# The inversion of each recurrence pair traced 6 to 10 weight units later, its transfers on GpSimd's queue

## The chip, the core and the metric

One core of one Trainium2 chip. The metric is the device time of one execution in microseconds, the median of three runs. The engines are TensorE (PE; its weight loads run beside it as PEld), VectorE (DVE), ScalarE (ACT), GpSimd (POOL) and SyncE (SP), whose queue issues the kernel's DMAs. Each engine works through its own list of instructions in order.

## What is computed

Two transformer blocks, one after the other, on 256 tokens of width 2048, in float32. The first block's mixer has a stick-breaking attention, a forgetting attention and a recurrence of 16 heads of 64 with a decay, and a gated sum of the three; an MLP follows. The second block has pooling, a latent attention, a memory attention and a gated convolutional MLP. The change touches the recurrence only:

```python
def frame(state, inp):
    r_t, w_t, k_t, v_t, kk_t, kka_t = inp
    sa = jnp.einsum('bhvk,bhk->bhv', state, kk_t)
    state = (state * w_t[:, :, None, :] - sa[..., None] * kka_t[:, :, None, :]
             + v_t[..., None] * k_t[:, :, None, :])
    return state, jnp.einsum('bhvk,bhk->bhv', state, r_t)
```

## The kernel before

**Products.** Nearly all time goes into products of the 256 tokens with weights that are read once. A weight unit is 128 x 1024 float32 (512 KB): `load` (L214) has SP fetch it into `raw`, ACT copy its high part to `hi` (L227) and DVE compute the rest `lo = raw - hi` (L228). Each of the three has three buffers. `lin_t` (L232) goes over output columns in steps of 256 and, within them, over units of four 128-row slices; each slice takes a matmul with `hi` (512 columns, both parts of the tokens) and one with `lo` (256). `lin_n` (L264) is the same with tokens as rows. Results stand in PSUM banks `m` (four) until an eviction takes them (`halves`, L287: ACT writes `hv`, DVE adds). Everything else on PE uses four further banks `s` (`side`, L155).

**Order.** The code is traced in program order; a planner then lays out a list for each engine by readiness and priority, where the trace order is the priority and the weight copies of `load` go far ahead (L226). On the chip an engine follows that list, whatever is ready.

**The recurrence.** `rwkv(q)` (L710) does a quarter of the heads: three products (k, r, v; twelve units), then two pairs of heads in `rwkv_pair` (L368), each with two chunks of 128 tokens for two heads, so four 128 x 128 systems. A pair has

- a head (L372 to L433): decays by scan and exponentials (`cs`, `E`, `Ei`), the scaled operands `AR`, `Bt`, `Kt`, their transposes, and four score matrices into `SM`;
- `k.flush()` (L435), which traces the finish of the pair before;
- the inversion: DVE masks the 16 x 16 diagonal blocks into `X` and reduces them to `mc` (L444, L446). SP writes `mc` to a DRAM tile `md` (32 KB, L448) and reads it back broadcast to all partitions as `mb` (512 KB, L450), after `md` has landed. Fifteen steps `zw`, `zc` on DVE (L454 to L457) invert the blocks, L458 spreads them into `Z`; transposes and small matmuls on PE with copies on ACT and DVE between them (L459 to L495) extend that to 128 x 128;
- the rest: two chunks `R`, `U`, `ys` (L498 to L532), the bonus `pb`, `y2` and the gate `pg`, `gg` (L535 to L543);
- `finish` (L545), which normalises `ys` and writes `yc`.

Tiles have one buffer unless `bufs` says otherwise: `X`, `Z`, `zc`, `mb`, `rk`, `kk` have one, `SM`, `AR`, `vt` two.

**Around it.** The quarters stand between other products: rwkv(0), an attention (24 units, then its softmax), rwkv(1), the other attention, rwkv(2), branch(0) (40 units), rwkv(3), flush, then branch(1) (40 units) and branch(2) (L750 to L800). PE can take the products that follow in the trace while a pair waits.

Of the kernel before, what the change touches and what calls it, by code (L numbers as in the profile page):

```python
# [10 lines left out]
F32 = mybir.dt.float32  # L11
# [113 lines left out]
class K:  # L125
    def __init__(self, ctx, tc):
        self.tc, self.nc, self.ctx = tc, tc.nc, ctx
        nc = tc.nc
        self.v, self.a, self.g, self.pe = nc.vector, nc.scalar, nc.gpsimd, nc.tensor
        pool = lambda name, bufs, **k: ctx.enter_context(tc.tile_pool(name=name, bufs=bufs, **k))  # L130
        self.cp = pool("cp", 1)
        self.wr = pool("wr", 3)
        self.wh = pool("wh", 3)
        self.wl = pool("wl", 3)
        self.ev = pool("ev", 2)
        self.dp = pool("dp", 2, space=bass.MemoryType.DRAM)
# [4 lines left out]
        self.finish = None  # L141
# [24 lines left out]
    def tt(self, out, a, b, op):  # L166
        self.v.tensor_tensor(out=out, in0=a, in1=b, op=op)  # L167
# [46 lines left out]
    def load(self, parts, kt, nc_):  # L214

        raw = self.wr.tile([P, 1024], F32, tag="raw", name=self.nm("raw"), align_bytes=LINE)
        hi = self.wh.tile([P, 1024], F32R, tag="hi", name=self.nm("hi"), align_bytes=LINE)
        lo = self.wl.tile([P, 1024], F32R, tag="lo", name=self.nm("lo"), align_bytes=LINE)
        r3 = raw[:, : kt * nc_].rearrange("p (k n) -> p k n", k=kt)
        h3 = hi[:, : kt * nc_].rearrange("p (k n) -> p k n", k=kt)  # L220
        l3 = lo[:, : kt * nc_].rearrange("p (k n) -> p k n", k=kt)
        for c, ap in parts:
            n = ap.shape[1]
            self.nc.sync.dma_start(r3[:, :, c : c + n], ap.rearrange("(k p) n -> p k n", p=P))
        rr, hh, ll = raw[:, : kt * nc_], hi[:, : kt * nc_], lo[:, : kt * nc_]
        with self.tc.high_priority(offset=3000):  # L226
            self.act(hh, rr, AF.Copy)  # L227
            self.tt(ll, rr, hh.bitcast(F32), ALU.subtract)  # L228
        return h3, l3


    def lin_t(self, w, x, kts, cols, evac, row0=0, xk0=0, segs=None):  # L232
# [7 lines left out]
        for c0, width in cols:  # L240
            ntile = (width + P - 1) // P
            banks = [self.pm.tile([P, 512], F32, tag="m", name=self.nm("m")) for _ in range(ntile)]
            for k0, kt in kts:
# [6 lines left out]
                for j in range(ntile):  # L250
                    m = min(P, width - j * P)
                    for k in range(kt):
# [7 lines left out]
                                start=False, stop=last)  # L260
            for j in range(ntile):
                evac((c0, j), min(P, width - j * P), banks[j])

    def lin_n(self, w, x, kts, cols, evac, row0=0, xk0=0):  # L264


        for c0, width in cols:
            banks = [self.pm.tile([P, 512], F32, tag="m", name=self.nm("m")) for _ in range(2)]
            step = max(1, 1024 // width)
            for k0 in range(0, kts, step):  # L270
# [3 lines left out]
                for t in range(2):  # L274
                    o = banks[t][:, :width]
                    for k in range(kt):
# [42 lines left out]
def rwkv_quarter(k, pool, q, zk, lw, sg1, sg2, w_up, a_up, g_up, yc):  # L319
# [40 lines left out]
    def pairs(zr, zv):  # L360
        for j in range(2):
# [6 lines left out]
def rwkv_pair(k, tl, j, zr, zk, zv, sg, aa, rin, omka, col, gu1, gu2, sg1, sg2, yc):  # L368

# [31 lines left out]
    eif = Ei.rearrange("p c t -> p (c t)")  # L401
    k.stt(Bt, kk, 1.0 / SC, eif, ALU.mult, ALU.mult)
# [3 lines left out]
    k.stt(Kt, kp, 1.0 / SC, eif, ALU.mult, ALU.mult)  # L406
    rk = tl([P, 256], "rk")
# [12 lines left out]
    KT0 = tl([P, P], "KT0")  # L420
    BT0 = tl([P, P], "BT0")
# [13 lines left out]
    k.flush()  # L435
# [4 lines left out]
    Z = tl([P, 4, P], "Z")  # L440
# [11 lines left out]
    zc = tl([P, 4, NB], "zc")  # L452
    k.v.tensor_copy(zc, C["eyeb"].unsqueeze(1).to_broadcast([P, 4, NB]))
    for u in range(NB - 1):  # L454
        w = tl([P, 4, NB], "zw", bufs=2)[:, :, u + 1 :]
        k.tt(w, mb[:, u, :, u + 1 :], zc[:, :, u : u + 1].to_broadcast([P, 4, NB - 1 - u]), ALU.mult)
        k.tt(zc[:, :, u + 1 :], zc[:, :, u + 1 :], w, ALU.subtract)  # L457
    k.tt(blocks(Z), zc.unsqueeze(2).to_broadcast([P, 4, P // NB, NB]), bm, ALU.mult)  # L458
    px = k.side()  # L459
    for i in range(4):  # L460
        k.tp(px[:, i * P : (i + 1) * P], Z[:, i])
    k.act(flat(X), px, AF.Copy)


    half = lambda z, n, o: z.rearrange("p a (b o n) -> p a b o n", o=2, n=n)[:, :, :, o, :]
    wide = lambda z, n: z.rearrange("p (a b n) -> p a b n", a=4, n=n)
    xe, zo, te = half(X, NB, 0), half(Z, NB, 1), half(k.T, NB, 0)
    pt = k.side()[:, :256]
    for i in range(4):
        k.mm(pt[:, i * 64 : (i + 1) * 64], SM[:, i, 0, :], xe[:, i])  # L470
    k.tt(te, wide(pt, NB), C["lev16"].unsqueeze(1).to_broadcast([P, 4, 64]).rearrange("p a (b n) -> p a b n", n=NB),
         ALU.mult)
# [24 lines left out]

    ys = tl([P, 4, 64], "ys", bufs=2)  # L498
    S0 = tl([P, P], "S0")
    k.v.memset(S0, 0.0)  # L500
    for c in range(2):
        pr = k.side()
        if c == 1:
            k.mm(pr[:, :P], AR[:, 1, 0, :], S0, start=True, stop=False)
        for e in range(2):
            i, hs = 2 * c + e, slice(64 * e, 64 * e + 64)
            k.mm(pr[:, hs], SM[:, i, 2, :], vt[:, c, hs], start=c == 0, stop=c == 0 or e == 1)
        R = tl([P, P], "R")
        k.act(R, pr[:, :P], AF.Copy)
        pu = k.side()  # L510
        for e in range(2):
            hs = slice(64 * e, 64 * e + 64)
            k.mm(pu[:, hs], Z[:, 2 * c + e], R[:, hs])
        U = tl([P, P], "U")
        k.act(U, pu[:, :P], AF.Copy)
        if c == 0:
            pS = k.side()
# [10 lines left out]
        for e in range(2):
            i, hs = 2 * c + e, slice(64 * e, 64 * e + 64)
            k.mm(py[:, hs], SM[:, i, 3, :], vt[:, c, hs], start=c == 0, stop=False)  # L530
            k.mm(py[:, hs], SM[:, i, 1, :], U[:, hs], start=False, stop=c == 0 or e == 1)
        k.act(ys[:, 2 * c : 2 * c + 2].rearrange("p e d -> p (e d)"), py[:, :P], AF.Copy)  # L532


    pb = k.side()  # L535
    k.mm(pb[:, :256], brk, rk)
    y2 = tl([P, 256], "y2", bufs=2)
    k.tt(y2, pb[:, :256], zv, ALU.mult)
    pg = k.side()
    k.mm(pg[:, :256], gu1, sg1, start=True, stop=False)  # L540
    k.mm(pg[:, :256], gu2, sg2[:32], start=False, stop=True)
    gg = tl([P, 256], "gg", bufs=2)
    k.act(gg, pg[:, :256], AF.Copy)  # L543

    def finish():  # L545
# [115 lines left out]
def mixer(k, a, xhl):  # L661
# [651 lines left out]
```

## Time and profile before

| | us |
|---|---|
| median of 3 runs | 2752.08 (2749.4 to 2753.53) |
| the profiled execution | 2750.6 |
| its span, first to last instruction | 2748.4 |

The profile is of one execution. Busy time of PE is modelled from pipelined matmuls. A row of a table by windows gives, after its length, the busy time of PE, PEld, DVE, ACT and POOL. PEclk is the share of TensorE's full clock that was granted, over the stretch. "Idle before" is the time an engine stood before an instruction, and the releaser is what it waited for. The line of an instruction is often that of a helper (L160 matmul, L164 transpose, L167 tensor_tensor, L179 activation), so the tile names tell more.

### The profile page before, as it was taken

To read this page: it belongs to the slowest core of one execution; us is meant where nothing else is said; L and a number is where in the kernel's file an instruction comes from. 1 tells how busy PE (TensorE), PEld (TensorE's weight loads), DVE (VectorE), ACT (ScalarE), POOL (GpSimd) and SP (SyncE) were. 2 spreads that over 40 slices of the span, in tenths; PEclk is the share of its full clock that TensorE was granted. 3 is DMA by queue.
4 is the path that set the end of the run, shared out by engine and by line. 5 is a ranking of instruction groups with operands and counts; after the bars stand their busy time and mean duration, and the time that the engine had idled before them with its cause. 6 is when DMAs were issued, how large, how long until landed. Compare 5 with 4: busy or idle time off the path is not lost.

```text
span 2748.4 us, 38434 instructions
## 1 busy us (share of the span) xinstructions
PE 2682.7 (98%) x14588; PEld 2261.9 (82%) x14588; DVE 1734.2 (63%) x2985; ACT 1390.1 (51%) x2245; POOL 37.1 (1%) x36
## 2 busy tenths in 40 slices
PE   7999999999999999999999999999999999999999
PEld 6777787887888888888888888878788888888887
DVE  5657576567666566455565555757767567757764
ACT  7345364453555664444344444766655445535543
POOL 0000000000000000000000000000000000000000
PEclk9999999999999999999999999999999999999999
DMA  6445444464566756665665665554456566666655
GB/s 186 131 130 141 111 128 129 143 168 126 152 189 208 263 175 186 192 191 187 195 186 192 191 185 194 178 155 134 135 163 186 192 190 185 189 194 185 188 187 183
DMA packets 390232, 475.69 MB, mean 173 GB/s; under 512 B 20112, under 2 KB 306832, under 8 KB 390048
## 3 DMA queue, kind: packets, MB, share of 16 engines
q1 hardware_dynamic: 390016, 473.18, 56.6%
q8 instruction: 114, 1.87, 0.3%
q14 instruction: 70, 0.57, 0.1%
q0 software_dynamic: 32, 0.07, 0.0%
HBM read 470.82 MB, written 2.36 MB: 172 GB/s over the span
## 4 chain that ended last, share of the span: by engine, by line
PE 81%; issue 5%; DVE 5%; DMA 3%; ACT 1%; POOL 0%; SPq 0%; POOLq 0%; DVEq 0%; ACTq 0%
PE m L160 75%; PE s L160 5%; DMA mb<-md 2%; DVE lo L167 2%; PE s L164 1%; ACT hi L179 1%; DVE zw L167 1%; DVE zc L167 1%; DMA mt<-in_mem 0%; DMA mt<-in_memT 0%; DVE SM L167 0%; DVE Z L167 0%; POOL rs L196 0%; DVE zz L167 0%; DMA raw<-in_w_in 0%
## 5 line engine op out<-in xcount | busy, mean ns | idle before, releaser
L167 DVE TENSOR_TENSOR lo<-raw,hi 128x1024 fp32r<-128x1024 f32 (+1 forms) x874 | 1062.8, 1217 | 757.8 <-ACT hi L179 754.5
L179 ACT ACTIVATE hi<-raw 128x1024 fp32r<-128x1024 f32 (+1 forms) x874 | 919.9, 1053 | 1040.6 <-PE m L160 793.2
L160 PE MATMUL m<-uhl,hi 128*128 128x512 f32 (+1 forms) x1456 | 528.4, 403 | 2.4 <-DVE zz L167 2.4
L160 PE MATMUL m<-x3hl,hi 128*128 128x512 f32 x1408 | 497.8, 399 | 0.0
L160 PE MATMUL m<-uhl,lo 128*128 128x256 f32 (+1 forms) x1456 | 419.2, 288 | 13.5 <-DVE lo L167 13.5
L160 PE MATMUL m<-x3hl,lo 128*128 128x256 f32 x1408 | 395.5, 281 | 0.0
L160 PE MATMUL m<-A,hi 128*128 128x512 f32 x1024 | 362.0, 399 | 1.8 <-DVE A L170 1.8
L160 PEld LDWEIGHTS m<-uhl,hi 128*128 128x128 f32 (+1 forms) x1456 | 277.0, 190 | 65.8 <-DVE zz L167 3.4
L160 PEld LDWEIGHTS m<-x3hl,hi 128*128 128x128 f32 x1408 | 264.6, 188 | 66.1
L160 PE MATMUL m<-hi,B 128*128 128x512 f32 x1024 | 315.9, 389 | 0.0
L160 PEld LDWEIGHTS m<-uhl,lo 128*128 128x128 f32 (+1 forms) x1456 | 277.8, 191 | 17.5 <-DVE lo L167 15.1
L160 PE MATMUL m<-A,lo 128*128 128x256 f32 x1024 | 287.3, 281 | 0.0
L160 PEld LDWEIGHTS m<-x3hl,lo 128*128 128x128 f32 x1408 | 266.0, 189 | 0.1
L160 PEld LDWEIGHTS m<-A,hi 128*128 128x128 f32 x1024 | 192.0, 188 | 49.2 <-DVE A L170 2.4
L160 PEld LDWEIGHTS m<-hi,B 128*128 128x128 f32 x1024 | 192.2, 188 | 40.0
L160 PE MATMUL m<-hi,h 128*128 128x512 f32 x704 | 217.4, 389 | 0.0
L160 PE MATMUL m<-lo,B 128*128 128x512 f32 x512 | 199.2, 389 | 0.0
L160 PEld LDWEIGHTS m<-A,lo 128*128 128x128 f32 x1024 | 193.3, 189 | 0.8 <-DVE lo L167 0.2
L160 PEld LDWEIGHTS m<-hi,h 128*128 128x128 f32 x704 | 132.1, 188 | 27.6
L179 ACT ACTIVATE hv<-m 128x256 f32<-128x256 f32 x323 | 119.8, 373 | 56.2 <-PE m L160 53.6
L167 DVE TENSOR_TENSOR zz<-m,hv 128x256 f32<-128x256 f32 x307 | 126.8, 417 | 17.6 <-ACT hv L179 17.6
L160 PE MATMUL m<-lo,h 128*128 128x512 f32 x352 | 137.0, 389 | 0.0
(373 smaller groups left out, 3011.1 us busy)
## 6 DMA issues: line engine op xcount, KB each, us to landing
raw<-in_w_in SPq DMA_DIRECT2D x220, 512.0 KB, 3.6
raw<-in_w_mlp_up SPq DMA_DIRECT2D x128, 512.0 KB, 3.6
raw<-in_w_mlp_down SPq DMA_DIRECT2D x128, 512.0 KB, 3.7
raw<-in_w_gate SPq DMA_DIRECT2D x88, 512.0 KB, 3.5
raw<-in_w_up SPq DMA_DIRECT2D x88, 512.0 KB, 3.6
raw<-in_w_down SPq DMA_DIRECT2D x88, 512.0 KB, 3.6
raw<-in_w_out SPq DMA_DIRECT2D x32, 512.0 KB, 4.6
raw<-in_w_o SPq DMA_DIRECT2D x32, 512.0 KB, 3.6
```

Of the source, the lines that this page charges most:

```text
L160: self.pe.matmul(out, lhsT=lhsT, rhs=rhs, start=start, stop=stop)
L164: self.pe.transpose(out, in_, self.C["ident"][:n, :n])
L167: self.v.tensor_tensor(out=out, in0=a, in1=b, op=op)
L179: self.a.activation(out, in_, f, **k)
```

## The change

`rwkv_pair` keeps the head, then traces `pb`, `pg`, the mask and reduction and the two DMAs, now issued by GpSimd. All that follows becomes `solve()`, which is put on a list (`defer`) and traced after 6 further weight units for the first pair of a quarter and 10 for the second; a `tick()` after each unit of `lin_t` and `lin_n` counts down. Only the front of the list is looked at, so the first pair's finish is traced right after the second pair's solve, and the second's a unit later. `pairs` begins with `drain()`. The first `zc` is held behind the split `lo` of the unit traced last. `mb`, `KT0`, `BT0` get two buffers; `Ei` is written over `cs`, `rk` over `kk`, and the bonus goes straight to `yc`. The closing of the recurrence's pool moves behind branch(1).

```diff
-    def flush(self):
-        if self.finish is not None:
-            f, self.finish = self.finish, None
-            f()
+    def defer(self, units, f):
+        self.later.append([units, f])
+    def tick(self):
+        for e in self.later:
+            e[0] -= 1
+        while self.later and self.later[0][0] <= 0:
+            self.later.pop(0)[1]()
+    def drain(self):
+        while self.later:
+            self.later.pop(0)[1]()
...
+            self.last_lo = self.tt(ll, rr, hh.bitcast(F32), ALU.subtract)
...
+                self.tick()
...
     def pairs(zr, zv):
+        k.drain()
...
-    Ei = tl([P, 2, P], "Ei")
...
+    Ei = cs[:, :, 1:]
+    for c in range(2):
+        k.act(Ei[:, c], Ei[:, c], AF.Exp, scale=KAPPA, bias=bp[:, 1, c : c + 1])
...
-    rk = tl([P, 256], "rk")
+    rk = kk
...
-    KT0 = tl([P, P], "KT0")
-    BT0 = tl([P, P], "BT0")
+    KT0 = tl([P, P], "KT0", bufs=2)
+    BT0 = tl([P, P], "BT0", bufs=2)
...
-    k.flush()
+    pb = k.side()
+    k.mm(pb[:, :256], brk, rk)
+    k.tt(yc, pb[:, :256], zv, ALU.mult)
+    pg = k.side()
...
-    k.nc.sync.dma_start(md.rearrange("b (u n) -> (b u) n", u=NB), flat(mc))
-    mb = tl([P, NB, 4, NB], "mb")
-    k.nc.sync.dma_start(mb.rearrange("p u a t -> p (u a t)"),
+    k.nc.gpsimd.dma_start(md.rearrange("b (u n) -> (b u) n", u=NB), flat(mc))
+    mb = tl([P, NB, 4, NB], "mb", bufs=2)
+    k.nc.gpsimd.dma_start(mb.rearrange("p u a t -> p (u a t)"),
                         md.unsqueeze(1).to_broadcast([P // NB, NB, NB * 4 * NB]))
...
+    def solve():
+        zc = tl([P, 4, NB], "zc")
+        with k.tc.issue_after(k.last_lo.ins):
+            k.v.tensor_copy(zc, C["eyeb"].unsqueeze(1).to_broadcast([P, 4, NB]))
...
+        k.defer(1, lambda: finish(ys))
...
-    k.finish = finish
+    k.defer(6 + 4 * j, solve)
...
     rwkv(3)
-    k.flush()
-    rst.close()
     branch(1, a["w_branch_b"][0], ybT, 4)
+    k.drain()
+    rst.close()
```

## Rows read from the trace of the kernel before

**Rows 1.** The page: span, and busy time of each engine (share of the span).

```profile
span 2748.4 us, 38434 instructions
...
PE 2682.7 (98%) x14588; PEld 2261.9 (82%) x14588; DVE 1734.2 (63%) x2985; ACT 1390.1 (51%) x2245; POOL 37.1 (1%) x36
```

**Rows 2.** Windows by stage: from:to, length, busy us by engine (x count), PEclk, DMA.

```profile
75.00:195.00 120.00, 109.78 (x703) 89.79 (x702) 70.06 (x175) 45.45 (x79) 2.16 (x2) 0.97 0.45 124
...
235.00:360.00 125.00, 116.42 (x750) 95.14 (x748) 77.98 (x202) 48.14 (x89) 2.09 (x2) 0.97 0.46 125
...
398.00:512.00 114.00, 104.63 (x697) 87.57 (x696) 74.16 (x199) 46.15 (x90) 1.13 (x2) 0.94 0.45 125
512.00:598.00 86.00, 85.62 (x492) 73.86 (x491) 52.73 (x85) 47.43 (x78) 2.60 (x2) 1.00 0.61 174
598.00:715.00 117.00, 107.51 (x729) 89.32 (x728) 79.76 (x201) 49.88 (x96) 2.09 (x2) 0.97 0.45 124
```

**Rows 3.** Waits of PE, 75 to 715: us in total, times, longest.

```profile
PE m L160 <- DVE lo L167: 18.5, 8, 4.8
PE s L164 <- DVE Z L167: 14.4, 7, 3.3
```

**Rows 4.** Waits of DVE, 75 to 715.

```profile
DVE zw L167 <- DMA mb<-md: 41.3, 8, 7.1
```

**Rows 5.** Timeline of DVE, pair 0: start, us, instruction [idle before <-releaser].

```profile
86.86 1.05 DVE L446 TENSOR_REDUCE mc<-X 128x64 f32<-128x512 f32 x1
...
89.69 1.22 DVE L167 TENSOR_TENSOR lo<-raw,hi 128x1024 fp32r<-128x1024 f32 x1 [0.65 <-ACT hi L179]
...
92.48 1.23 DVE L167 TENSOR_TENSOR lo<-raw,hi 128x1024 fp32r<-128x1024 f32 x1 [1.22 <-ACT hi L179]
98.32 0.22 DVE L167 TENSOR_TENSOR zw<-mb,zc 128x60 f32<-128x60 f32 x1 [4.62 <-DMA mb<-md]
...
100.17 1.22 DVE L167 TENSOR_TENSOR lo<-raw,hi 128x1024 fp32r<-128x1024 f32 x1
...
109.23 1.22 DVE L167 TENSOR_TENSOR lo<-raw,hi 128x1024 fp32r<-128x1024 f32 x1
```

**Rows 6.** Timeline of SP's queue, same place: issues.

```profile
87.94 0.35 SPq L448 DMA_DIRECT2D md<-mc  x1
89.07 0.37 SPq L224 DMA_DIRECT2D raw<-in_w_in  x1
89.50 0.71 SPq L450 DMA_DIRECT2D mb<-md  x1
```

**Rows 7.** Timeline of PE, same place.

```profile
101.44 0.38 PE L160 MATMUL m<-uhl,lo 128*128 128x256 f32 x1 [1.26 <-DVE lo L167]
...
109.36 0.66 PE L164 MATMUL s<-idt,Z 128*128 128x128 f32 x4 [3.35 <-DVE Z L167]
```

**Rows 8.** Windows of 24 us after mc, pairs 4 and 7.

```profile
410.70:434.70 24.00, 19.31 (x99) 16.63 (x98) 14.44 (x42) 9.96 (x14) 0.00 (x0) 0.86 0.56 147
...
666.00:690.00 24.00, 19.98 (x111) 16.57 (x111) 19.39 (x55) 10.49 (x17) 0.00 (x0) 1.00 0.58 156
```

**Rows 9.** Tile rx, 58 to 142 (first and last start); DVE in a window.

```profile
L160 PE MATMUL s<-idt,rx x8: 272/275/377, 75.5 to 131.2; 128*128 128x128 f32 x8
L391 DVE COPY rx<-rin x4: 219/221/226, 63.2 to 78.8; 128x128 f32<-128x128 f32 x4
...
129.80:140.30 10.50, 8.57 (x24) 1.00 0.18 51
```

**Rows 10.** DMA issues by line: count, KB each, median us from issue to landing.

```profile
wua<-in_rwkv_w_up SPq DMA_DIRECT2D x4, 64.0 KB, 2.2
wua<-in_rwkv_a_up SPq DMA_DIRECT2D x4, 64.0 KB, 4.5
...
grow<-in_rows POOLq DMA_DIRECT2D x1, 64.0 KB, 3.9
```

**Rows 11.** Waits of SP's queue, 75 to 715.

```profile
SPq L448 <- DVE mc L446: 43.8, 6, 9.9
```

More of the change, by code (lines that the diff above doesn't have):

```diff
@@ L140, in __init__ @@
         self.abufs = 1
-        self.finish = None
+        self.later = []
+        self.last_lo = None
     def nm(self, s):
@@ L166, in tt @@
     def tt(self, out, a, b, op):
-        self.v.tensor_tensor(out=out, in0=a, in1=b, op=op)
+        return self.v.tensor_tensor(out=out, in0=a, in1=b, op=op)
     def stt(self, out, a, s, b, op0, op1):
@@ L453, in rwkv_pair @@
[L453 to L472, printed above, removed]
@@ L498, in rwkv_pair @@
[L498 to L517, printed above, removed]
+    def solve():
+        zc = tl([P, 4, NB], "zc")
+        with k.tc.issue_after(k.last_lo.ins):
+            k.v.tensor_copy(zc, C["eyeb"].unsqueeze(1).to_broadcast([P, 4, NB]))
+        for u in range(NB - 1):
+            w = tl([P, 4, NB], "zw", bufs=2)[:, :, u + 1 :]
+            k.tt(w, mb[:, u, :, u + 1 :], zc[:, :, u : u + 1].to_broadcast([P, 4, NB - 1 - u]), ALU.mult)
+            k.tt(zc[:, :, u + 1 :], zc[:, :, u + 1 :], w, ALU.subtract)
+        Z = tl([P, 4, P], "Z")
+        k.tt(blocks(Z), zc.unsqueeze(2).to_broadcast([P, 4, P // NB, NB]), bm, ALU.mult)
+        X = tl([P, 4, P], "X")
+        px = k.side()
+        for i in range(4):
+            k.tp(px[:, i * P : (i + 1) * P], Z[:, i])
+        k.act(flat(X), px, AF.Copy)
+        half = lambda z, n, o: z.rearrange("p a (b o n) -> p a b o n", o=2, n=n)[:, :, :, o, :]
+        wide = lambda z, n: z.rearrange("p (a b n) -> p a b n", a=4, n=n)
+        xe, zo, te = half(X, NB, 0), half(Z, NB, 1), half(k.T, NB, 0)
+        pt = k.side()[:, :256]
+        for i in range(4):
+            k.mm(pt[:, i * 64 : (i + 1) * 64], SM[:, i, 0, :], xe[:, i])
+        k.tt(te, wide(pt, NB), C["lev16"].unsqueeze(1).to_broadcast([P, 4, 64]).rearrange("p a (b n) -> p a b n", n=NB),
+             ALU.mult)
+        pz = k.side()[:, :256]
+        for i in range(4):
+            k.mm(pz[:, i * 64 : (i + 1) * 64], k.T[:, i], zo[:, i])
+        k.tt(zo, zo, wide(pz, NB), ALU.subtract)
+        px = k.side()
+        for i in range(4):
+            k.tp(px[:, i * P : (i + 1) * P], Z[:, i])
+        k.v.tensor_copy(xe, half(px.rearrange("p (a t) -> p a t", a=4), NB, 0))
+        for n in (32, 64):
+            T = tl([P, 4, n], f"T{n}")
+            pt, px, pz = (k.side()[:, : 4 * n].rearrange("p (a n) -> p a n", a=4) for _ in range(3))
+            for b in range(0, P, 2 * n):
+                lo, hi = slice(b, b + n), slice(b + n, b + 2 * n)
+                for i in range(4):
+                    k.mm(pt[hi, i], SM[lo, i, 0, hi], X[lo, i, lo])
+                k.act(T[hi], pt[hi], AF.Copy)
+                for i in range(4):
+                    k.mm(pz[lo, i], T[hi, i], Z[hi, i, hi])
+                if n == 32:
+                    for i in range(4):
+                        k.mm(px[hi, i], Z[hi, i, hi], T[hi, i])
+                    k.ts(X[hi, :, lo], px[hi], -1.0)
+                k.ts(Z[lo, :, hi], pz[lo], -1.0)
+        ys = tl([P, 4, 64], "ys", bufs=2)
+        S0 = tl([P, P], "S0")
+        k.v.memset(S0, 0.0)
+        for c in range(2):
+            pr = k.side()
+            if c == 1:
+                k.mm(pr[:, :P], AR[:, 1, 0, :], S0, start=True, stop=False)
+            for e in range(2):
+                i, hs = 2 * c + e, slice(64 * e, 64 * e + 64)
+                k.mm(pr[:, hs], SM[:, i, 2, :], vt[:, c, hs], start=c == 0, stop=c == 0 or e == 1)
+            R = tl([P, P], "R")
+            k.act(R, pr[:, :P], AF.Copy)
+            pu = k.side()
@@ L528, in rwkv_pair @@
[L528 to L545, printed above, removed]
+                k.mm(pu[:, hs], Z[:, 2 * c + e], R[:, hs])
+            U = tl([P, P], "U")
+            k.act(U, pu[:, :P], AF.Copy)
+            if c == 0:
+                pS = k.side()
+                for e in range(2):
+                    hs = slice(64 * e, 64 * e + 64)
+                    k.mm(pS[hs, :64], KT0[:, hs], vt[:, 0, hs], start=True, stop=False)
+                    k.mm(pS[hs, :64], BT0[:, hs], U[:, hs], start=False, stop=True)
+                for e in range(2):
+                    hs = slice(64 * e, 64 * e + 64)
+                    k.act(S0[hs, hs], pS[hs, :64], AF.Identity, scale=scend[hs, :1])
@@ new lines, in solve @@
+            py = k.side()
+            if c == 1:
+                k.mm(py[:, :P], AR[:, 1, 1, :], S0, start=True, stop=False)
+            for e in range(2):
+                i, hs = 2 * c + e, slice(64 * e, 64 * e + 64)
+                k.mm(py[:, hs], SM[:, i, 3, :], vt[:, c, hs], start=c == 0, stop=False)
+                k.mm(py[:, hs], SM[:, i, 1, :], U[:, hs], start=False, stop=c == 0 or e == 1)
+            k.act(ys[:, 2 * c : 2 * c + 2].rearrange("p e d -> p (e d)"), py[:, :P], AF.Copy)
@@ L547, in finish @@
+        k.defer(1, lambda: finish(ys))
+    def finish(ys):
         mv = tl([P, 4, 2], "mv")
@@ L789, in mixer @@
     rwkv(3)
-    k.flush()
+    branch(1, a["w_branch_b"][0], ybT, 4)
+    k.drain()
     rst.close()
-    branch(1, a["w_branch_b"][0], ybT, 4)
     hp = k.phase(k.rightctx, "mh", side="right")
```

46 lines of the change are left out of this document (9 added, 37 removed).

## The prediction

> **What bounds the kernel now.** I read the page first: TensorE (PE) is busy 98% of the span [rows 1], so only two things can be won: microseconds in which PE stands, and microseconds in which it runs slowly. The table by stages says where they are. The four stretches that hold a recurrence quarter (75 to 195, 235 to 360, 398 to 512, 598 to 715 us) have PE busy 109.78 of 120, 116.42 of 125, 104.63 of 114 and 107.51 of 117, so 10.22 + 8.58 + 9.37 + 9.49 = 37.7 us idle, and granted clocks of 0.97, 0.97, 0.94 and 0.97. The stretch 512 to 598, which has the same products but no inversion, stands only 0.38 us in 86 at clock 1.00 [rows 2]. So the recurrence costs idle time and clock, and a stretch without it shows what is attainable.
>
> Next, who ends PE's waits there: the low halves of the weights (lo) 18.5 us and the inverse Z 14.4 us, 32.9 of the 37.7 [rows 3]. Both are VectorE (DVE) results. DVE itself waits 41.3 us in eight waits of zw for the transfer mb<-md [rows 4], about as much. The timeline of pair 0 joins the two. The reduction mc starts at 86.86 and ends at 87.91; SP issues md at 87.94 and mb at 89.50 [rows 6]; zw, the first user of mb, begins at 98.32 after an idle of 4.62 [rows 5]. So the round trip takes 98.32 - 87.91 = 10.4 us, and the order on DVE was laid out for less. DVE works in order: the next weight split, which follows the one at 92.48 after the usual 2.8 us (89.69 to 92.48), runs only at 100.17. PE then stands 1.26 us for it and 3.35 us at Z [rows 7]: 4.61 us, DVE's 4.62 handed on. This is the mechanism: a late DMA at the head of DVE's queue starves PE.
>
> **The change part by part**, against the profiled execution (2750.6 us; span 2748.4, so 2.2 us lie around it; the median of the runs is 1.5 us more).
>
> Same work: matmuls, transposes, the 31 small DVE steps and Z are the same in number and size, so no engine gains busy time. Ei written over cs, rk over kk, yc in place of y2: no instruction more or less. The in-place Ei makes the second pair's scan wait until the first pair has used its Ei; that is some 2 us in a stretch where PE has products to run. I cost it at 0, with 0 to 1 us per quarter as bounds.
>
> The wait. Before, pair 1's head could not run while pair 0 waited: its first side product, s<-idt,rx, has its last run of pair 1 at 131.2 although its last input was written at 78.8 [rows 9]; I read this as the side banks being given out in the order of the trace, in which pair 0's whole inversion came first. After, pair 1's head is traced ahead of pair 0's inversion. While mb travels DVE has real work: in 129.80 to 140.30, which is pair 1's head without a full weight split but with pair 0's normalisation, it is busy 8.57 us [rows 9]. I take 6 to 8.6 us for the head. With three weight splits of 1.22 us [rows 5] that fall in the same time, 3.7 us, DVE is taken for 9.7 to 12.3 us after mc. The transfer takes 10.4 us now. So for pair 0 arrival and need come together; six units (6 x 2.8 = 17 us of PE time) help less than they seem to, as several units run ahead of mc already: weight splits go on at 89.69 and 92.48, right behind it. For pair 1, ten units, its zw also queues behind pair 0's chain (zc has one buffer), which takes 10 us from 98.32 to the transposes of Z near 109 [rows 5, 7], so mb is long there: wait 0, with 1 us per pair as the upper bound. The new order of zc behind a split adds no wait of its own: the split is needed by PE earlier than Z, and behind zc stand only the inversion's own steps and what was laid out later. The pool that closes after branch(1) in place of before it frees its memory later; its next user is branch(2), 40 units on, so 0.
>
> The queue. GpSimd's only DMA before, 64 KB, lands 3.9 us after issue; two of the same size on SP take 2.2 and 4.5 [rows 10]. So a transfer on GpSimd may be 0.6 us quicker or 1.7 us slower; two in a row, -1.2 to +3.4 us on 10.4. I take +1, the middle. On the other side mb no longer stands behind a weight load (issued at 89.07, just ahead of it [rows 6]), and SP loses its stop at md: it waited 43.8 us in six waits for mc with weight loads queued behind [rows 11]. Those loads have three buffers of slack, so I count nothing for it. On GpSimd's own queue the md and mb of pair 1 and the powers rs stand behind a waiting mb; rs is needed only by the finish, which is not among PE's two large waits [rows 3].
>
> The Trainium skill speaks against this part. "SBUF — State Buffer", sections "SBUF: two separate sides" and "Who interferes with whom", says that GpSimd writes the descriptors of its own DMAs and is locked out while DVE runs a copy or tensor_scalar in a two-port mode; a DMA from SP is immune. No row here shows it. By it each of the 16 issues could be late by one such copy, an estimate of 0.22 us by the copy rx [rows 9], so the sum would be 3.5 us higher if none of it were hidden.
>
> Residual wait of pair 0: between 0 (DVE taken for 12.3, mb there after 10.4) and 8 us (zw placed as early as now, 98.32 - 4.62 - 87.91 = 5.8 us after mc, and mb there after 10.4 + 3.4 = 13.8). I take 1.5, nearer the end where DVE has work, since that work stands ahead in the trace.
>
> Sum of the idle time: 37.7 now. Left over: 4 x 0.4 as in the stretch without an inversion, 4 x 1.5 for the first pairs: 7.6. Won: 30.
>
> The clock. Each of the stretches loses (1 - clock) x length: 0.03 x 120 + 0.03 x 125 + 0.06 x 114 + 0.03 x 117 = 17.7 us, as time at 1.2 in place of 2.4 GHz. It goes with the stalls: the 24 us after the mc of pair 4 have 4.69 us of idle time and run at 0.86; those of pair 7 have 4.02 and keep 1.00; the stretch without an inversion keeps 1.00 [rows 2, 8]. So idle time of this size can come with a lower clock and without one, but the clock never fell where there was none. With waits of 1.5 us most of it should return; I leave 4 us. Won: 13.5, bounds 0 to 17.7.
>
> Forecast: 2750.6 - 30 - 13.5 = 2707; with the median's 1.5 us about 2708.5 us.
>
> **The rivals.**
> (a) Half of it: only the second pairs get clear, and the first wait as now. Pairs 1, 3, 5, 7 should hold about half of the idle time and of the clock, as 4.69 and 4.02 us of idle time after an even and an odd pair suggest [rows 8]: (37.7 + 17.7) / 2 = 27.7, so 2723 + 1.5 = 2725; if the transfer is also 3.4 us slower, 4 x 3.4 comes back: 2738. For it: two weight splits run within 5 us of mc already, so units are ahead of the pair [rows 5]. Against it: 6 to 8.6 us of head stand ahead of zw.
> (b) No change: zw is placed as early in both pairs and waits as long, so the trace order moves and the machine order does not. 2752 +- 5. For it: the order of an engine is laid out by a forecast that was 4.6 us too short for this very transfer [rows 5]. Against it: two heads before the first inversion cannot be skipped.
> (c) Slower: DVE becomes the bound of the stretch. Both heads (6 to 8.6 us each) and two chains of 10 us now follow one another without the pause, with a weight split of 1.22 us in every unit. In the chain of pair 0 the splits already come 3.02 us apart ((109.23 - 100.17) / 3) against 2.8 outside it [rows 5], so 0.2 us per unit is late. Over some 25 units x 4 quarters that is 20 us, which the buffers mostly hide. It decides against the change when a unit is late by over 0.55 us, since 100 x 0.55 = 55 us is all there is to win; with one head step such as a mask of 0.7 us ahead of each split it is 100 x 0.7 - 55 = 15 us slower: 2767. Against it: DVE is busy only 70.06 of 120 us in the first stretch [rows 2], and splits come first in the order.
>
> **How the numbers follow.** Forecast 0.62, (a) 0.18, (b) 0.07, (c) 0.13. 0.2% is 5.5 us, about what a measurement of this kernel can tell from no change. Faster: 0.62 + 0.18 = 0.80; same 0.07; slower 0.13. Low end: all idle and clock won, 2750.6 - 37.7 - 17.7 = 2695, and 3 us for small waits that go along: 2692. High end: (a) with the slow transfer, 2738, and 4 x 1 us for the in-place Ei: 2742. Outside lie (b) and (c), 0.20.
>
> **What would show it.** Right: PE idle in the four stretches together near 8 us, PE's waits for lo and Z down from 32.9 us to a few, DVE's wait for mb only before the first zw of each quarter and under 2 us, the clock at 0.99 or more, md and mb on GpSimd's queue, s<-idt,rx of pair 1 some 10 us after pair 0's and not 55. Wrong: a wait of zw for mb of 4 us or more in the first pairs (a) or in all (b); PE waiting for lo with DVE busy all the while (c). The forecast falls above all if zw keeps its early place on DVE.

## The result, and the profile after

| | before | after |
|---|---|---|
| median of four runs on one chip | 2750.74 us | 2713.28 us (2710.17 to 2715.59) |
| after to before | | 0.9855, 95% interval 0.9843 to 0.9866 |
| the profiled execution | 2750.6 us | 2715.02 us |
| its span | 2748.4 us | 2713.3 us |

The change makes the kernel 1.45% faster, about 37 us. Forecast were 2708.5 us, in a range from 2692 to 2742.

Line numbers of the changed kernel are larger: matmul is L171 (before L160), transpose L175 (L164), the helper of `tensor_tensor` L178 (L167), the activation helper L190 (L179), `mc` L470, `md` L472, `mb` L474. First the table by stages, which answers to [rows 2] (from:to, length, busy time of PE, PEld, DVE, ACT and POOL with their counts, granted clock, DMA share, GB/s). The stretches start and end at the same work as there, so they are shorter:

```profile
73.50:193.00 119.50, 116.05 (x759) 95.94 (x758) 79.13 (x197) 52.17 (x89) 4.73 (x6) 1.00 0.50 137
230.00:345.00 115.00, 110.90 (x725) 90.72 (x724) 75.51 (x194) 46.12 (x85) 4.51 (x6) 1.00 0.48 131
382.00:490.00 108.00, 103.41 (x707) 86.12 (x706) 76.09 (x199) 47.43 (x93) 4.51 (x6) 0.98 0.47 128
490.00:570.00 80.00, 79.58 (x457) 68.60 (x456) 47.50 (x71) 44.37 (x71) 1.64 (x1) 1.00 0.63 179
570.00:680.00 110.00, 107.00 (x715) 88.97 (x714) 80.61 (x213) 50.47 (x100) 4.51 (x6) 0.97 0.45 126
```

In the four stretches with a recurrence PE now stands 3.45 + 4.10 + 4.59 + 3.00 = 15.1 us; it was 37.7. The clock falls short by 0.02 x 108 + 0.03 x 110 = 5.5 us; it was 17.7. That is 22.6 and 12.2, together 34.8 of the 35.6 us between the two profiled executions.

What PE waits for in 60 to 720 us answers to [rows 3] (total us, times, longest), and DVE's only wait for `mb` there to [rows 4]:

```profile
PE s L175 <- DVE Z L178: 7.5, 4, 2.2
PE s L175 <- DVE ys L178: 2.6, 4, 0.8
PE s L171 <- DVE Bt L181: 2.6, 3, 0.9
PE s L175 <- DVE Kt L181: 1.0, 2, 0.7
PE m L171 <- DVE zz L178: 0.7, 1, 0.7
```

```profile
DVE zw L178 <- DMA mb<-md: 0.2, 1, 0.2
```

The wait for `lo`, 18.5 us before, is gone. The wait for Z has halved, one for each quarter, always at its first pair. DVE's wait for `mb` went from 41.3 us to 0.2. New are small waits for steps of the second head (`Bt`, `Kt`); those for a step of the finish (`ys`) have grown from 0.5 us in one to 2.6 in four.

The timeline of DVE at pair 0 (start, duration, instruction, idle time before it and its releaser) answers to [rows 5]:

```profile
84.49 1.04 DVE L470 TENSOR_REDUCE mc<-X 128x64 f32<-128x512 f32 x1
...
87.56 0.42 DVE L181 SCALAR_TENSOR_TENSOR Bt<-kk,cs 128x256 f32<-128x256 f32 x1
87.90 1.22 DVE L178 TENSOR_TENSOR lo<-raw,hi 128x1024 fp32r<-128x1024 f32 x1
...
94.14 1.03 DVE L470 TENSOR_REDUCE mc<-X 128x64 f32<-128x512 f32 x1
95.95 1.23 DVE L178 TENSOR_TENSOR lo<-raw,hi 128x1024 fp32r<-128x1024 f32 x1 [0.78 <-ACT hi L190]
...
97.43 0.18 DVE L479 COPY zc<-C 128x64 f32<-128x64 f32 x1
97.65 0.22 DVE L178 TENSOR_TENSOR zw<-mb,zc 128x60 f32<-128x60 f32 x1
...
107.63 0.17 DVE L178 TENSOR_TENSOR zc<-zc,zw 128x4 f32<-128x4 f32 x1
108.71 1.23 DVE L178 TENSOR_TENSOR lo<-raw,hi 128x1024 fp32r<-128x1024 f32 x1 [0.90 <-PE m L171]
109.85 0.68 DVE L178 TENSOR_TENSOR Z<-zc,C 128x512 f32<-128x512 f32 x1
```

Between the two reductions `mc` lies most of the head of pair 1 (its two scans `cs`, at 81.59 and 82.50, come just ahead of the first), where before there was an idle 4.62 us ahead of `zw`. The first `zw` starts 97.65 - 85.53 = 12.1 us after `mc` and waits for nothing. GpSimd's queue at the same place shows why: `md` is issued at 85.84, `mb` at 88.06, and the eight `mb` take a median 7.8 us from issue to landing, so this one is there near 96.

```profile
85.84 0.74 POOL L472 DMA_DIRECT2D md<-mc  x1 [23.82 <-DVE scend L181]
88.06 0.63 POOL L474 DMA_DIRECT2D mb<-md  x1 [1.48 <-DMA md<-mc]
```

```profile
mb<-md POOLq DMA_DIRECT2D x8, 512.0 KB, 7.8
md<-mc POOLq DMA_DIRECT2D x8, 32.0 KB, 1.9
```

What is left at this place is in the last three DVE rows above. The chain is done at 107.80, but ahead of Z in DVE's list stands a split that stands still for 0.90 us and then takes 1.23; Z is written at 110.53, and PE's transposes have waited for it:

```profile
110.59 0.66 PE L175 MATMUL s<-idt,Z 128*128 128x128 f32 x4 [1.55 <-DVE Z L178]
```

### The profile page after: what moved, and what is told of

Its sections match the earlier page's. It is cut to its first block, busy times and chain, and to the rows that moved or that the text cites. A ratio compares the mean times of both kernels' runs of the same rounds, so it can differ in the third digit from the quotient of the medians.

```text
span 2713.3 us, 38492 instructions
## 1 busy us (share of the span) xinstructions
PE 2671.1 (98%) x14588; PEld 2258.4 (83%) x14588; DVE 1735.5 (64%) x2985; ACT 1393.3 (51%) x2245; POOL 46.9 (2%) x52
## 4 chain that ended last, share of the span: by engine, by line
PE 69%; issue 5%; DVE 1%; ACT 0%; POOL 0%; POOLq 0%; DVEq 0%; ACTq 0%
PE m L171 68%; PE s L175 0%; PE s L171 0%; DVE lo L178 0%; ACT hi L190 0%; DVE xres L181 0%; POOL qrs L207 0%; POOLq L1327 0%; DVE A L181 0%; POOL krs L207 0%; DVE acc L178 0%; ACT L190 0%; ACT jk L190 0%; DVE qr L178 0%; DVE sm_mx L620 0%
## 5 line engine op out<-in xcount | busy, mean ns | idle before, releaser
L178 DVE TENSOR_TENSOR lo<-raw,hi 128x1024 fp32r<-128x1024 f32 (+1 forms) x874 | 1063.2, 1217 | 790.8 <-ACT hi L190 784.9
L190 ACT ACTIVATE hi<-raw 128x1024 fp32r<-128x1024 f32 (+1 forms) x874 | 920.4, 1054 | 1020.9 <-PE m L171 791.6
L171 PE MATMUL m<-uhl,hi 128*128 128x512 f32 (+1 forms) x1456 | 524.6, 400 | 0.7 <-DVE zz L178 0.7
L171 PE MATMUL m<-x3hl,hi 128*128 128x512 f32 x1408 | 495.4, 397 | 0.0
L171 PE MATMUL m<-uhl,lo 128*128 128x256 f32 (+1 forms) x1456 | 416.3, 286 | 0.0
L171 PE MATMUL m<-x3hl,lo 128*128 128x256 f32 x1408 | 395.2, 281 | 0.0
L171 PE MATMUL m<-A,hi 128*128 128x512 f32 x1024 | 360.8, 397 | 1.8 <-DVE A L181 1.8
L171 PEld LDWEIGHTS m<-uhl,hi 128*128 128x128 f32 (+1 forms) x1456 | 273.3, 188 | 60.8 <-DVE zz L178 1.4
L171 PEld LDWEIGHTS m<-x3hl,hi 128*128 128x128 f32 x1408 | 264.3, 188 | 63.7
L171 PE MATMUL m<-hi,B 128*128 128x512 f32 x1024 | 315.9, 389 | 0.0
L171 PE MATMUL m<-A,lo 128*128 128x256 f32 x1024 | 287.2, 281 | 0.0
L171 PEld LDWEIGHTS m<-uhl,lo 128*128 128x128 f32 (+1 forms) x1456 | 275.3, 189 | 3.4 <-issue 2.3
L171 PEld LDWEIGHTS m<-x3hl,lo 128*128 128x128 f32 x1408 | 266.0, 189 | 0.1
L171 PEld LDWEIGHTS m<-A,hi 128*128 128x128 f32 x1024 | 191.8, 188 | 48.2 <-DVE A L181 2.4
L171 PEld LDWEIGHTS m<-hi,B 128*128 128x128 f32 x1024 | 192.3, 188 | 39.9
L171 PE MATMUL m<-hi,h 128*128 128x512 f32 x704 | 217.1, 389 | 0.0
L171 PE MATMUL m<-lo,B 128*128 128x512 f32 x512 | 199.2, 389 | 0.0
L171 PEld LDWEIGHTS m<-A,lo 128*128 128x128 f32 x1024 | 193.3, 189 | 0.7 <-DVE lo L178 0.2
L171 PEld LDWEIGHTS m<-hi,h 128*128 128x128 f32 x704 | 132.2, 188 | 27.4
L190 ACT ACTIVATE hv<-m 128x256 f32<-128x256 f32 x323 | 120.7, 375 | 60.8 <-PE m L171 57.9
L178 DVE TENSOR_TENSOR zz<-m,hv 128x256 f32<-128x256 f32 x307 | 126.9, 418 | 19.6 <-ACT hv L190 19.5
L171 PE MATMUL m<-lo,h 128*128 128x512 f32 x352 | 137.0, 389 | 0.0
```

What stands on the lines that cost most here:

```text
L171: self.pe.matmul(out, lhsT=lhsT, rhs=rhs, start=start, stop=stop)
L178: return self.v.tensor_tensor(out=out, in0=a, in1=b, op=op)
L190: self.a.activation(out, in_, f, **k)
```

## The experiments

The theory T: the gain is the round trip `mc` - `md` - `mb` leaving the head of DVE's list, because the second head is traced ahead of the first inversion and fills DVE meanwhile. Its rivals: the queue (SP no longer stops at `md`), the small edits, the units, and the new order as such.

One view serves for all: the window 60 to 720 us of each kernel, in which PE's idle time is 660 less its busy time; "clock" is the granted clock in it. Ratios are to runs of the kernel before on the same chip; its row gives the range of its medians on four chips.

| kernel | median us | ratio, 95% interval | PE idle us | clock |
|---|---|---|---|---|
| before | 2750.74 to 2753.16 | 1 | 38.3 | 0.97 |
| before_pool_queue | 2758.72 | 1.0022 (1.0010 to 1.0034) | 48.8 | 0.97 |
| after_drain_each | 2760.16 | 1.0026 (1.0013 to 1.0039) | 46.7 | 0.97 |
| before_own_row | 2720.27 | 0.9881 (0.9857 to 0.9905) | 17.4 | 0.99 |
| before_no_trip | 2705.35 | 0.9820 (0.9794 to 0.9845) | 10.2 | 1.00 |
| after_units_0 | 2723.94 | 0.9892 (0.9864 to 0.9919) | 18.2 | 0.98 |
| after_no_issue_after | 2722.82 | 0.9880 (0.9855 to 0.9905) | 21.8 | 0.99 |
| after_long_trip | 2724.74 | 0.9901 (0.9879 to 0.9922) | 24.5 | 0.98 |
| after | 2713.28 | 0.9855 (0.9843 to 0.9866) | 15.8 | 0.99 |
| after_again | 2718.06 | 0.9867 (0.9845 to 0.9890) | 15.7 | 0.99 |
| after_z_later | 2711.10 | 0.9848 (0.9833 to 0.9863) | 13.8 | 1.00 |
| after_sp_queue | 2708.05 | 0.9840 (0.9816 to 0.9864) | 10.9 | 1.00 |
| sp_queue_z_later | 2710.81 | 0.9845 (0.9825 to 0.9866) | 11.1 | 1.00 |
| units_10_16 | 2719.41 | 0.9878 (0.9859 to 0.9897) | 19.2 | 1.00 |

### What is the wait worth?

**before_no_trip**, the kernel before with a table in place of `mb`:

```diff
-    mb = tl([P, NB, 4, NB], "mb")
-    k.nc.sync.dma_start(mb.rearrange("p u a t -> p (u a t)"),
-                        md.unsqueeze(1).to_broadcast([P // NB, NB, NB * 4 * NB]))
+    mb = k.mt
...
+    k.mt = tl([P, NB, 4, NB], "mt")
+    k.nc.sync.dma_start(k.mt.rearrange("p u a t -> p (u a t)"), w_in[:P, :NB * 4 * NB])
```

> Part left out: the inversion reads a table of weights that is loaded once, in place of mb; md is still written by SP, mb is not read back, everything else is the kernel before. Theory T (the change gains by taking the 10.4 us round trip mc - md - mb off the head of DVE's queue): DVE's waits for mb (41.3 us) are gone without anything being reordered, PE's waits for lo and Z fall from 32.9 to under 12 us, time 2707 to 2722 us. Rival Q (SP's stop at md and the weight loads behind it carry the loss; the stop is kept here): 2740 to 2755. Rival O (the order of the two heads and the side banks carry it, and the trip is only what the profile names): 2735 to 2750.

2705.35 us, a little below T's range. But the run took away more than the wait. Right after pair 0's reduction DVE is already at the second step on Z (90.92), and Z of pair 1 is written at 104.00, ahead of the reduction of pair 1 at 115.77:

```profile
86.37 1.04 DVE L446 TENSOR_REDUCE mc<-X 128x64 f32<-128x512 f32 x1
87.33 1.22 DVE L167 TENSOR_TENSOR lo<-raw,hi 128x1024 fp32r<-128x1024 f32 x1
90.92 0.42 DVE L167 TENSOR_TENSOR Z<-Z,s 128x256 f32<-128x256 f32 x1 [1.26 <-PE s L160]
...
104.00 0.69 DVE L167 TENSOR_TENSOR Z<-zc,C 128x512 f32<-128x512 f32 x1 [1.23 <-PE s L160]
...
115.77 1.03 DVE L446 TENSOR_REDUCE mc<-X 128x64 f32<-128x512 f32 x1
```

A table that depends on nothing lets the chain of 31 steps run ahead of `mc`. The run also leaves out the 512 KB of each `mb`, and its weight loads land sooner. The longest took 5.1 us from issue to landing, against 8.7 us in the kernel before and 7.1 to 9.5 us in every other run. The first row is of before, the second of before_no_trip (loads of `raw`, 60 to 720 us):

```profile
DMA to landing us min/median/max: 3.4/3.6/8.7
DMA to landing us min/median/max: 3.4/3.6/5.1
```

So this is the price of trip, chain and transfer together, not of the trip; a second run was needed.

**before_own_row**, in which each partition takes its own row of `mc`, so that the spread over the partitions is left out:

```diff
-        k.tt(w, mb[:, u, :, u + 1 :], zc...
+        k.tt(w, mc[:, :, u + 1 :], zc...
```

> Part changed: each of the 15 zw steps reads its own row of mc in place of mb; md and mb are still transferred by SP, mb is read by nobody, and the chain still begins with mc, so the round trip alone leaves the path (the table of the run before_no_trip let the chain run ahead of mc altogether). T: with the trip gone and nothing reordered, DVE waits 0 for mb, PE's waits for lo and Z fall from 32.9 to under 15 us, 2707 to 2725 us. Rival O (most of the gain of the changed kernel is in the new order, which also keeps two chains off the same stretch): 2730 to 2745 us.

2720.27 us, in T's range: the trip alone, with the trace order kept and `md` and `mb` still transferred, is worth 1.2% (0.95 to 1.43), 33 us. PE's wait for `lo` is gone altogether, so the 18.5 us of [rows 3] were the trip handed on. The wait for Z stays near its 14.4 us; the third row is PE's at pair 0, 3.35 us before:

```profile
PE s L164 <- DVE Z L167: 12.8, 8, 2.3
PE m L160 <- DVE zz L167: 2.9, 4, 1.0
...
99.47 1.08 PE L164 MATMUL s<-idt,Z 128*128 128x128 f32 x4 [1.92 <-DVE Z L167]
```

So most of Z's wait is not the trip's: with `mc` at hand the chain still comes too late for PE, in every pair. The run also speaks against rival Q: SP still stands 39.7 us in eight stops at the issue of `md` (53.3 in eight before).

### Queue and small edits

**before_pool_queue** and **after_sp_queue** exchange the queue of `md` and `mb`, nothing else:

```diff
-    k.nc.sync.dma_start(md...
+    k.nc.gpsimd.dma_start(md...
...
-    k.nc.sync.dma_start(mb...
+    k.nc.gpsimd.dma_start(mb...
```

> The kernel before with md and mb issued by GpSimd, nothing else. T: the trip stays at the head of DVE's queue; DVE waits 35 to 55 us for mb, time 2747 to 2762 us (trip -1.2 to +3.4 us for eight pairs). Q: SP no longer stops for 43.8 us, so the weight loads come in time and 20 to 40 us are won: 2710 to 2730.

> The changed kernel with md and mb on SP's queue again. T: the trip lies beside pair 1's head on either queue: 2710 to 2718 us, DVE's waits for mb under 3 us. Q: most of the gain goes, 2735 to 2752, with SP waiting some 40 us for mc and PE waiting for lo again.

The first is as T expects; the second lies 2 us below T's range and far from Q's. By itself the queue costs 0.22%. DVE's wait for `mb` is (53.6 - 41.3) / 8 = 1.5 us longer a pair, and PE's for `lo` 11 us longer in all ([rows 3, 4] have 18.5 and 41.3):

```profile
PE m L160 <- DVE lo L167: 29.5, 8, 6.3
PE s L164 <- DVE Z L167: 15.9, 8, 3.5
```

```profile
DVE zw L167 <- DMA mb<-md: 53.6, 8, 8.5
```

The issue tells part of it. On GpSimd `md` is issued 0.31 us after `mc` and `mb` 2.22 us after that; on SP 0.03 and 1.56 us [rows 5, 6]. In the changed kernel SP's queue does no harm: 2708.05 us, PE's idle time 10.9 in place of 15.8 us, and Z's wait is shorter:

```profile
PE s L175 <- DVE Z L178: 3.1, 3, 1.6
```

**after_drain_each**, the changed kernel with only the trace order undone:

```diff
-    k.defer(6 + 4 * j, solve)
+    solve()
```

> The changed kernel, with each pair's inversion traced right behind its own head, so ahead of the next pair's head; in-place tiles, early gate products, doubled buffers and GpSimd's queue stay. T: the trip is at the head of DVE's queue again, DVE waits 35 to 60 us for mb, 2745 to 2768 us. Rival E (the small edits in the head carry part of the gain): DVE waits as long, but 2713 to 2740 us.

As T expects: 2760.16 us, all of the gain is gone, and the kernel stands where before_pool_queue stands (1.0026 and 1.0022). DVE waits for `mb` again as before:

```profile
DVE zw L178 <- DMA mb<-md: 46.4, 8, 7.0
```

In the old order the in-place `Ei` and `rk`, the early gate products and the doubled buffers are together worth nothing that these intervals show; the trace order carries the change. Whether the new order needs the doubled buffers wasn't tried.

### Heads, units and the rule on zc

**after_units_0** traces both inversions right behind the two heads:

```diff
                       col, gu1[...], gu2[...], sg1, sg2, yc[:, 2 * q + j])
+        k.drain()
```

> The changed kernel with both inversions traced right behind the two heads (no units between). T (as the prediction has it, the head of pair 1 covers the trip of pair 0 and the chain of pair 0 that of pair 1, 6 and 10 units help little): 2711 to 2722 us, DVE waiting under 8 us for mb. Rival U (it is the units that keep zw from the head of the queue): DVE waits 15 us or more for mb, 2725 to 2750.

2723.94 us, between the two: 2 us above what I expected of T, and 1 us below U. The waits for `mb` are T's, 6.0 us in four, one at each first pair (1.5, 2.0, 0.9 and 1.7 us):

```profile
DVE zw L178 <- DMA mb<-md: 6.0, 4, 2.0
```

From 1.0026 with the heads in the old order to 0.9892 the second head brings 1.3%. To the units some 0.3% would be left, but the intervals overlap (0.9864 to 0.9919 against 0.9843 to 0.9866, and 0.9845 to 0.9890 for the repetition below). That the units help is seen in the profiles only: DVE's waits for `mb` are 6.0 us without them and 0.2 with them. **units_10_16**, on SP's queue, asks for more of the same:

```diff
-    k.defer(6 + 4 * j, solve)
+    k.defer(10 + 6 * j, solve)
```

> The changed kernel with SP's queue (2708 us in its own run) and 10 and 16 units in place of 6 and 10. T (mb is there by 6 and 10 units, later units win nothing more): 2704 to 2712 us. Rival U (each further unit takes load off the crowded stretch behind the heads, as from 0 to 6 and 10 units): 2695 to 2703 us. Rival L (too late: the side buffers and the finish come into the next stretch): 2713 us or more.

2719.41 us: T and U fail, and the time is L's. Against 6 and 10 units on the same queue (0.9840) the intervals overlap a little, but PE's idle time is 19.2 us in place of 10.9. L's reason isn't shown. Z's wait, 3.1 us there, now comes in all eight pairs:

```profile
PE s L175 <- DVE Z L178: 9.5, 8, 2.5
```

**after_no_issue_after**:

```diff
-        with k.tc.issue_after(k.last_lo.ins):
+        if True:
             k.v.tensor_copy(zc, ...)
```

> The changed kernel without the rule that zc comes behind the latest weight split. T as in the prediction (that rule adds no wait of its own, and the head of pair 1 covers the trip without it): 2709 to 2717 us, waits for mb under 8 us. Rival W (the rule holds zc back and puts a split ahead of Z): Z is written earlier, PE's waits for Z under 3 us, 2702 to 2708 us. Rival H (the rule is what keeps zw off the head of the queue): DVE waits 15 us or more for mb, 2720 to 2745 us.

2722.82 us (2713.2 to 2726.55), above T's 2717 and against W: without the rule PE's wait for Z grows to 10.3 us, and DVE waits 5.2 us in four for `mb`. That is T's wait, not H's 15 us, though the time lies in H's range. The profiles speak for the rule, with an idle time of 21.8 us without it and 15.8 with it; the times don't show it, as the intervals overlap.

### How much slack is left?

**after_long_trip** puts one hop more into the trip:

```diff
+    me = k.dp.tile([P // NB, NB * 4 * NB], F32, tag="me", name=k.nm("me"))
+    k.nc.gpsimd.dma_start(me, md)
...
-                        md.unsqueeze(1).to_broadcast(...
+                        me.unsqueeze(1).to_broadcast(...
```

> The changed kernel with one hop more: GpSimd copies md to a second DRAM tile and mb is read from that, some 2 to 5 us per pair by the landing of 1.8 us and the issue of 0.6 us of md. T (pair 0's mb lands within about 2 us of need, pair 1's long before): the first pairs of four wait 2 to 5 us each for mb, 8 to 20 us in all, the second pairs 0; with the clock 2720 to 2740 us. Rival S (slack is left in both pairs): under 3 us of waits, 2710 to 2718 us. Rival B (both pairs are tight): eight waits, 2735 us or more.

`mb` is issued 91.10 - 86.12 = 5.0 us after `mc` in place of 2.5. The time, 2724.74 us, is T's; the waits are only half so. DVE waits three times, 4.2 us: 0.33 and 2.42 in two first pairs (quarters 1 and 2, counted from 0), 1.43 in a second one. The profiled execution took 2732.19 us, 7.5 us more than the median. In it PE's idle time is 8.7 us more than in the changed kernel, most of it at Z and what follows:

```profile
PE s L175 <- DVE Z L178: 9.0, 4, 4.4
PE s L171 <- ACT X L190: 4.2, 2, 2.9
```

So the slack differs: none at the first pair of quarter 2, where DVE waits 0.22 us without the hop already, about 2.2 and 1.1 us in the two pairs of quarter 1, and more than 2.5 us in the others, if the hop adds 2.5 us to each. The hop costs about 0.3% (0.9901 against 0.9867 for the changed kernel on the same chip, with overlapping intervals). That every second pair's `mb` is there long before was too much said.

### What is left at Z

**after_z_later** traces the transposes of Z a unit after Z:

```diff
+        k.later.insert(0, [1, lambda: rest(Z)])
+
+    def rest(Z):
         X = tl([P, 4, P], "X")
         px = k.side()
```

> The changed kernel, with the transposes of Z and all behind them traced one unit after the mask that makes Z. T (the 7.5 us of waits for Z left in the changed kernel are a matter of order: PE reaches the transposes before DVE, behind a weight split, has written Z): PE's waits for Z under 2.5 us, 2703 to 2709 us with the clock it takes along. Rival R (the chain of pair 0 itself is late, PE then stands at the next reader): 2711 to 2718 us with the same idle time at other lines.

2711.10 us with 6.4 us of waits for Z (7.5 before the edit): T's expectation fails. R's time holds, but the wait stays at Z and doesn't move to the next reader. Tracing the reader later doesn't help, as it is the chain on DVE that is late. The timeline of the changed kernel shows its cause at the first pairs: a split that waits 0.90, 1.41, 1.97 and 1.68 us (quarters 0 to 3) stands in DVE's list ahead of Z or of the chain's last steps, and PE's waits for Z there are 1.55, 2.06, 2.21 and 1.71. The rows of quarters 1 and 2:

```profile
261.64 1.23 DVE L178 TENSOR_TENSOR lo<-raw,hi 128x1024 fp32r<-128x1024 f32 x1 [1.41 <-ACT hi L190]
262.79 0.69 DVE L178 TENSOR_TENSOR Z<-zc,C 128x512 f32<-128x512 f32 x1
...
416.25 1.22 DVE L178 TENSOR_TENSOR lo<-raw,hi 128x1024 fp32r<-128x1024 f32 x1 [1.97 <-ACT hi L190]
```

It is the pattern of [rows 5] in small, with a late `hi` where the late `mb` was. (In quarter 0 the profile names a matmul as what the split waited for, but there too `hi` ends only 0.04 us before the split.) Why `hi` is late the timeline of ACT shows, for quarters 1 to 3: it waits for its weight load.

```profile
260.55 1.06 ACT L190 ACTIVATE hi<-raw 128x1024 fp32r<-128x1024 f32 x1 [3.88 <-DMA raw<-in_w_in]
415.16 1.06 ACT L190 ACTIVATE hi<-raw 128x1024 fp32r<-128x1024 f32 x1 [3.95 <-DMA raw<-in_w_branch_a]
605.30 1.06 ACT L190 ACTIVATE hi<-raw 128x1024 fp32r<-128x1024 f32 x1 [3.18 <-DMA raw<-in_w_branch_b]
```

The four loads in question are issued 1.8 to 4.1 us behind the second pair's `mb` and take 7.5, 8.0, 6.9 and 6.1 us to land; between 500 and 520 us, without an `mb`, loads take 3.4 to 3.6. On SP's queue the same four take 7.5, 7.0, 5.0 and 4.2 us, and PE's waits for Z are 1.63, 1.09, 0.35 and none. So what is left at Z goes with weight loads that travel beside the next pair's `mb`, and less of it on SP's queue. That it is this transfer that slows them rests on before_no_trip, the only run without it, where no load took over 5.1 us; no run takes it out of the changed kernel.

**after_again** and **sp_queue_z_later**, the changed kernel beside it with the two edits that had come out lowest:

> The changed kernel itself, as the measure for the next one: 2710 to 2716 us.

> The changed kernel with SP's queue and the transposes of Z traced a unit later, the two edits that came out lowest. If both were real and add up: 2702 to 2707 us; if only SP's queue counts: 2706 to 2711; if neither: 2711 to 2716 us, as after_again beside it.

2718.06 and 2710.81 us, with overlapping intervals. after_again is 2 us above its expectation. The profiles agree with each other better than the times: PE's idle time is 15.8 and 15.7 us in two profiles on GpSimd's queue (13.8 with the edit at Z), 10.9 and 11.1 on SP's. So SP's queue is the better one by 3 to 5 us of idle time, and the edit at Z adds nothing to it. A version faster than the changed kernel beyond the measurement isn't shown.

## Why the prediction was right

**The mechanism** held. "A late DMA at the head of DVE's queue starves PE": before_own_row takes the trip away and the wait for `lo` vanishes; after_drain_each puts it back and loses everything. One reading went too far: that PE's 1.26 us at `lo` and 3.35 us at Z are together DVE's 4.62 us handed on. Without the trip PE still waits 1.92 us for Z at pair 0 and 12.8 us in all, so the equal sums were in part chance, and the trip's share was `lo`. That Z's wait halved all the same is the new order's doing: the second pairs no longer wait, and in after_drain_each it is 17.4 us.

**The wait** (pair 0). DVE was to be taken 9.7 to 12.3 us after `mc`; from 85.53 to 97.43 it is 11.9 us, with two splits where three were counted, pauses of 0.54 and 0.78 us, and a head of 9.7 us (85.44 to 95.17; one split and the first pause are in it). Arrival and need come together within 0 to some 2.5 us, as after_long_trip shows. The residual of 1.5 us a first pair came out at 7.5 / 4 = 1.9, but for another reason: not `mb`, for which DVE waits 0.2 us, but a split ahead of Z, held by a late weight load. A size that was right by luck. I had counted the weight load ahead of `mb`, not those behind it.

**Rows that the forecast named**: waits for `lo` and Z "from 32.9 us to a few" (7.5), the wait for `mb` under 2 us a quarter (0.2 in all), `md` and `mb` on GpSimd's queue, `s<-idt,rx` of pair 1 some 10 us after pair 0's (82.97 after 74.24, 8.7 us): right. The clock "at 0.99 or more" holds in two of the four stretches (1.00, 1.00, 0.98, 0.97). PE idle "near 8 us": 15.1.

**The term that was mis-sized** is that idle time, which is nearly all of the distance between 43.5 us forecast and 35.6 had (22.6 won for 30). Left over were to be 4 x 1.5 + 4 x 0.4 = 7.6 us; measured are 15.1. Z makes up 1.5 of the difference; `ys`, `Bt` and `Kt`, 2.6 + 2.6 + 1.0 = 6.2 us, make up nearly all the rest. None of the three is among the rows of before that I built on, and I counted the heads at nothing beyond the in-place `Ei`. At pair 0 `Bt` isn't held by `Ei`: DVE is busy without a pause from 84.49 to 87.98, with `mc` of pair 0 ahead of the second head's steps, while PE's last matmul ended at 87.12:

```profile
88.04 1.13 PE L171 MATMUL s<-AR,Bt 64*128 64x256 f32 x6 [0.92 <-DVE Bt L181]
```

It is rival (c) in small: two heads in a row make DVE the bound for 1 us a quarter. after_drain_each, with the in-place `Ei` but the heads apart, has no wait for `Bt` or `Kt`. It does wait for `ys`, 2.1 us in three, so that part isn't the heads'; its cause stays open. The second mis-sized term is the clock: 5.5 us lost where 4 were left, so 12.2 won for 13.5 (17.7 less 4 is 13.7; the sum took 13.5).

**The queue** was costed at +1 us a trip (-1.2 to +3.4); before_pool_queue has +1.5. What I didn't carry into the sum is what the queue does to the rest: on SP's queue the same kernel has 5 us less idle time, though DVE waits for `mb` only 0.2 us on GpSimd's. Most of it is the wait for Z, 3.1 in place of 7.5 us, which goes with the sooner weight loads above. The rule of the Trainium skill ("SBUF — State Buffer", "Who interferes with whom"), that DVE's copies lock out GpSimd's descriptor writes, would have added up to 3.5 us, an estimate from 16 issues. No row here shows an issue held up: the eight issues of `mb` take 0.613 to 0.627 us, those of `md` 0.559 to 0.745. Only three of the sixteen have a copy or tensor_scalar of DVE beside them (0.74, 0.61 and 0.60 us), and 0.74 us is also what the first issue takes in before_pool_queue, without one. So this case could hardly have shown the rule.

```profile
L474 POOL DMA_DIRECT2D mb<-md x8: 613/616/627, 88.1 to 595.0; - x8
```

**What was counted at nothing**: SP's stop at `md` of 43.8 us [rows 11] was worth little, as said: before_pool_queue removes it and is slower, with a longer trip in it, and before_own_row keeps most of it and gains 33 us. The small edits: nothing, as said (after_drain_each). The rule on `zc` "adds no wait of its own": right, and by the profiles it takes some away. "Six units help less than they seem to": the second head brings about four fifths of the gain; the units' part is within the intervals.

**The rivals.** (a) fell: no first pair waits for `mb` over 0.22 us. (b) fell. (c) decides nothing, but its small form is what the forecast missed.

## What to carry to other kernels

When an in-order engine stands at a DMA, price the trip from the instruction that starts it to the one that needs it, and look for work of the same engine that can be traced in between; one other pair's head covered 10 us here, and that was nearly all of the gain. Then ask what the cover itself makes late, since steps that ran alone now stand behind one another, and what the transfer makes late: the weight loads beside it took 6.1 to 8.0 us here in place of 3.5. To price a wait by an experiment, replace the data and keep the dependence and the transfer, or the planner moves the whole chain and the run prices something else.

## What I had not expected of the hardware

The clock did not follow the size of a stall here. The changed kernel and its repetition have nearly the same waits (7.5 and 7.8 us for Z, 2.6 and 2.5 for `Bt`), yet of three stretches of 20 us the granted clock was 1.00, 0.91 and 0.83 in one execution and 0.91, 0.83 and 0.91 in the other, with PE idle 1.7 to 2.5 us in each. The first fence is of after, the second of after_again:

```profile
259.00:279.00 20.00, 17.94 (x159) 14.54 (x158) 14.09 (x47) 6.95 (x13) 0.00 (x0) 1.00 0.43 126
413.00:433.00 20.00, 17.79 (x142) 15.12 (x140) 14.20 (x46) 7.95 (x14) 0.00 (x0) 0.91 0.50 148
608.00:628.00 20.00, 18.29 (x136) 15.17 (x134) 13.32 (x40) 6.76 (x13) 0.00 (x0) 0.83 0.37 106
```

```profile
259.00:279.00 20.00, 17.53 (x144) 14.51 (x142) 13.19 (x42) 6.65 (x12) 0.00 (x0) 0.91 0.38 109
413.00:433.00 20.00, 17.56 (x114) 14.85 (x112) 12.59 (x43) 7.13 (x12) 0.00 (x0) 0.83 0.53 149
608.00:628.00 20.00, 18.10 (x141) 15.38 (x140) 13.44 (x42) 8.95 (x15) 0.00 (x0) 0.91 0.47 144
```

Over whole executions of the changed kernel the granted clock was 0.997 and 0.998 in the two slower ones (2715.02 and 2715.59 us), 0.999 and 1.000 in the two faster ones (2710.17 and 2711.53). In units_10_16 19.2 us of idle time cost no clock (1.00), in after_units_0 18.2 us cost 0.02 of it. So in a forecast a stall's own length can stand as a number, and what it does to the clock only as a range.
